# A two-layer decoder trunk: the modulation loads of both feed-forwards move from SyncE's DMA queue to GpSimd's

## The chip, the cores and the metric

The kernel runs on one core of a Trainium2 chip. The metric is the device time of one execution in microseconds (us), the median of several runs. A profile is one further execution, recorded by the hardware profiler; its own time is given beside its span.

## The reference

Two layers work on x (512 positions, 1024 features, float32). The first mixes positions by stick-breaking attention, the second by attention over 128 keys that an indexer selects; each is followed by a gated feed-forward with a causal convolution of width 3. Each of the four sub-layers is normalised, shifted, scaled and gated by vectors that come from one condition vector c:

```python
cond = silu(c)
for i in range(2):
    mod = cond @ ada_w[i] + ada_b[i]                 # 1024 x 6144
    sh1, sc1, g1, sh2, sc2, g2 = split(mod, 6)
    h = rms_norm(x, norm_mix[i]) * (1 + sc1) + sh1
    x = x + g1 * (stick_breaking(h) if i == 0 else dsa(h))
    h = rms_norm(x, norm_ffn[i]) * (1 + sc2) + sh2
    u = conv3(h @ ffn_w_up[i]) + conv_b              # 512 x 5632
    gate, val = split(u, 2)
    x = x + g2 * ((silu(gate) * val) @ ffn_w_down[i])
```

The product `cond @ ada_w[1]` of the second layer is what the moved loads feed.

## The kernel before, in words

Activations are kept transposed: features lie on the 128 partitions, the 512 positions along the free axis. All weights lie in one array `wst` of chunks of 128 x 1024 float32, 512 KB each. A weight is used as the sum of a high part (rounded to a shorter float format, by ScalarE) and a low part (the rest); TensorE multiplies high by high, high by low and low by high. So each chunk is loaded as `raw` (`chunk_raw`, L613, on SyncE's queue, six buffers) and split: ScalarE copies it into `whi`, and then either VectorE subtracts into `wlo` (L653, L1535), or ScalarE writes the negated high part and GpSimd issues a DMA that adds the chunk from memory to it (L662, `add_up` L1543, `add_half` L1554, `add_down` L1732). GpSimd issues other accumulating DMAs too (L1579, L1714, L1752). GpSimd's engine does nothing else in a feed-forward.

The modulation of the second layer is not computed by TensorE. For each of 48 columns a chunk `ada` is loaded, and VectorE multiplies it by `cond` (the same on all partitions) and sums along the row (`dot`, which calls `ada_dot`, L722). 33 of these dots are run in the first layer's feed-forward and 8 in that of the second (`FFN_DOTS`), where the gate that they make is wanted only by the down projection's additions; the other 7 are run elsewhere and are not touched. In a feed-forward the tile `ada` has one buffer, so a load waits until the dot before has read it.

The order of a feed-forward's instructions is set by a planner (`ffn_plan`): it holds jobs with an engine, a duration, what they come after and when they are due, plays them forward with one queue per engine, and `ffn_layer` then calls the functions of class `do` in the order of the planned starts. A load is there a job of SyncE's (`load`), an accumulation one of GpSimd's; the dots are due at equal distances (`DOT_SPAN`). Each engine runs its own instructions in the order in which they were called. Ahead of the planned part stand the first columns of the up projection (`pt_first`, then `pt_u`, L1622 and L1626), whose four last accumulations are issued at L662. TensorE's later products are `pt_a`, `pt_b` and `pt_d` (L1649, L1653, up) and `pt_d` (L1741, down). What a product has written is read by ScalarE (L1489) and, for the convolution, twice by VectorE (L1494), which frees its bank; three banks serve `pt_u`.

Of the kernel before, what the change touches and what calls it, by code (L numbers as in the profile page):

```python
# [525 lines left out]
def chunk_order():  # L526
    keys = []
    for l in range(DEPTH):
        for g in range(6):
            keys += [("ada", l, g, k) for k in range(KT)]  # L530
    for p in range(PAIRS):
        keys += [("q", p), ("k", p)]
    for g in range(4):
        keys += [("v", g, h) for h in range(2)]
    for nm in ("o", "do"):
        for g in range(2):
            keys += [(nm, g, m) for m in range(4)]
    for l in range(DEPTH):
        for j in range(FT):
            keys += [("up", l, j, 0), ("up", l, j, 1)]  # L540
        for r in range(3):
            keys += [("dn", l, r, m) for m in range(KT)]
        keys += [("dn", l, 3, m) for m in range(4)]
    keys += [("qi", i) for i in range(4)] + [("kw",), ("lat",)]
    keys += [("dq", h) for h in range(HEADS)]
    keys += [("uv",)]
    keys += [("bt", n, i) for n in range(3) for i in range(2)]
    return {k: i for i, k in enumerate(keys)}


CH = chunk_order()
# [22 lines left out]
def kernel_body(ctx, tc, xT, wst, cst, smalls, crow, ccol, relb, outT):  # L574
    nc = tc.nc
    act, dve, pe, pool = nc.scalar, nc.vector, nc.tensor, nc.gpsimd
# [900 lines left out]
    def ffn_layer(l, first, man):  # L1477
        with ExitStack() as st:
# [3 lines left out]
            A, R, W, Y, dn, pt, T, half, t1, whole, t4s = {}, {}, {}, {}, {}, {}, {}, {}, {}, {}, {}  # L1482
# [41 lines left out]
            class do:  # L1524
# [240 lines left out]

                def load_ada(*d):
                    R[d] = fp.tile([P, D], F32, name="ada", bufs=1)
                    nc.sync.dma_start(R[d], wst[CH[("ada",) + d]])

                def dot(n, g, f):  # L1770
                    ada_dot(mod[n][:, g * KT + f:g * KT + f + 1], R[n, g, f])
# [816 lines left out]
```

## Time and profile before

| | |
|---|---|
| time, median of 3 runs | 1208.68 us (1208.6 to 1208.86) |
| the profiled execution | 1209.77 us, span 1208.0 us |
| granted TensorE clock | 1.000 |
| busy: TensorE | 1201.4 us, 99% |
| busy: VectorE, ScalarE, GpSimd | 1021.0, 804.7, 240.2 us |
| DMA moved | 226.73 MB, mean 188 GB/s |
| first feed-forward | about 279 to 583 us |
| second feed-forward | about 882 to 1205 us |

A row of a timeline gives the start and the duration in us, the engine, the line, the operation, the tile written and those read, how many like instructions were merged, and in brackets the idle time before it and what ended that. SPq is SyncE's queue, where DMAs are issued; POOL is GpSimd. A row of issues gives the size of each DMA and the median time from issue to landing. A row of waits gives the total, the number and the longest.

### The profile page before, as it was taken

How to read it: one execution, taken by the hardware profiler on the slowest of the kernel's cores; microseconds unless marked ns; L12 is line 12 of the kernel's file. 1: busy time of each engine (PE TensorE's matmuls, PEld its weight loads, DVE VectorE, ACT ScalarE, POOL GpSimd, SP SyncE). 2: the span in 40 equal slices, each digit the busy share in tenths (PEclk: the TensorE clock that was granted, in tenths of full speed). 3: DMA queues.
4: the chain of work that ended last, by engine and by line, in shares of the span. 5: the costliest groups of instructions: out<-in, count | busy, mean ns of one | idle time of the engine just before them, and what ended most of it. 6: DMA issues, size and time to landing. Idle time of an engine off the chain costs nothing.

```text
span 1208.0 us, 18307 instructions
## 1 busy us (share of the span) xinstructions
PE 1201.4 (99%) x6500; PEld 1006.1 (83%) x6500; DVE 1021.0 (85%) x1739; ACT 804.7 (67%) x1393; POOL 240.2 (20%) x284
## 2 busy tenths in 40 slices
PE   9999999999999999999999999999999999999998
PEld 6888788788898998898888778777888888888887
DVE  5898888988999988999798895678989898888883
ACT  5588786368666676666567458774786677677660
POOL 0001100001111111111000457881012122212110
PEclk9999999999999999999999999999999999999999
DMA  9778897629789898896611362346498888788662
GB/s 374 253 204 230 219 250 236 205 90 227 185 221 277 223 250 215 239 273 167 192 53 40 99 156 67 101 129 190 137 236 203 228 186 205 183 182 191 157 147 87
DMA packets 82947, 226.73 MB, mean 188 GB/s; under 512 B 16924, under 2 KB 20252, under 8 KB 82856
## 3 DMA queue, kind: packets, MB, share of 16 engines
q1 hardware_dynamic: 61920, 170.21, 43.1%
q0 software_dynamic: 20912, 55.33, 25.9%
q8 instruction: 51, 0.84, 0.3%
q14 instruction: 40, 0.33, 0.1%
q10 hardware_dynamic: 24, 0.02, 0.0%
HBM read 212.62 MB, written 2.16 MB: 178 GB/s over the span
## 4 chain that ended last, share of the span: by engine, by line
PE 92%; DMA 3%; DVE 1%; POOL 1%; issue 1%; ACT 1%; SPq 0%; POOLq 0%; DVEq 0%; ACTq 0%
PE pt_d L1741 16%; PE pt_a L1653 8%; PE pt_u L1622 6%; PE pt_a L1649 5%; PE pt_d L1653 4%; PE pt_u L1626 3%; PE pt_d L1649 3%; PE pt_l L694 2%; PE pt_l L696 2%; PE pt_l L695 2%; PE pt_qk L694 2%; PE pt_qk L696 2%; PE pt_qk L695 2%; PE pt_b L1653 2%; DMA raw<-wst 2%; PE pt_fv L1099 2%
## 5 line engine op out<-in xcount | busy, mean ns | idle before, releaser
L1741 PE MATMUL pt_d<-actlo,dnhi 128*128 128x512 f32 x288 | 112.8, 392 | 0.0
L1741 PE MATMUL pt_d<-acthi,dnhi 128*128 128x512 f32 x288 | 112.7, 391 | 0.0
L1531 ACT ACTIVATE whi<-raw 128x1024 fp32r<-128x1024 f32 x72 | 75.8, 1054 | 30.0 <-PE pt_a L1653 13.3
L644 ACT ACTIVATE whi<-raw 128x1024 fp32r<-128x1024 f32 x80 | 84.2, 1052 | 4.8 <-DMA raw<-wst 2.0
L662 POOL DMA_DIRECT2D wlo<-wst x23 | 19.9, 864 | 282.3 <-DVE hh L806 131.3
L1622 PE MATMUL pt_u<-hh,whi 128*128 128x512 f32 x320 | 75.8, 389 | 0.0
L1741 PE MATMUL pt_d<-acthi,dnlo 128*128 128x512 f32 x288 | 73.5, 391 | 0.0
L1622 PEld LDWEIGHTS pt_u<-hh,whi 128*128 128x128 f32 x320 | 60.0, 188 | 12.6 <-issue 0.2
L1543 POOL DMA_DIRECT2D wlo<-wst x37 | 32.2, 869 | 169.7 <-ACT wlo L1539 65.5
L1741 PEld LDWEIGHTS pt_d<-actlo,dnhi 128*128 128x128 f32 x288 | 54.2, 188 | 10.2
L1741 PEld LDWEIGHTS pt_d<-acthi,dnhi 128*128 128x128 f32 x288 | 54.2, 188 | 10.1
L1741 PEld LDWEIGHTS pt_d<-acthi,dnlo 128*128 128x128 f32 x288 | 53.1, 188 | 10.3
L1649 PE MATMUL pt_a<-hh,whi 128*128 128x512 f32 x228 | 61.4, 391 | 0.1
L1349 DVE TENSOR_TENSOR_SCAN mz<-mz,diag 128x768 f32<-128x768 f32 (+1 forms) x32 | 47.6, 1486 | 15.1 <-ACT mz L1343 14.9
L1653 PE MATMUL pt_a<-hh,wlo 128*128 128x256 f32 x360 | 57.4, 282 | 0.0
L1653 PEld LDWEIGHTS pt_a<-hh,wlo 128*128 128x128 f32 x360 | 53.1, 190 | 4.5
L722 DVE SCALAR_TENSOR_TENSOR raw<-raw,cond 128x1024 f32<-128x1024 f32 x46 | 54.8, 1219 | 1.4 <-ACT cond L1167 1.3
L1964 DVE CUSTOM_DVE_ANT_0 L<-z,L,cols 128x128 f32<-128x128 f32 (+3 forms) x60 | 32.4, 547 | 27.2 <-PE tr L2267 17.6
L653 DVE TENSOR_TENSOR wlo<-raw,whi 128x1024 fp32r<-128x1024 f32 x42 | 51.6, 1228 | 3.3 <-ACT whi L644 2.9
L1554 POOL DMA_DIRECT2D whi<-wst x30 | 26.0, 866 | 132.3 <-ACT whi L1551 76.0
L722 DVE SCALAR_TENSOR_TENSOR ada<-ada,cond 128x1024 f32<-128x1024 f32 x41 | 49.9, 1218 | 2.5 <-DMA ada<-wst 2.5
L694 PE MATMUL pt_q<-hh,whi 128*128 128x512 f32 x128 | 51.8, 405 | 0.0
(423 smaller groups left out, 3796.7 us busy)
## 6 DMA issues: line engine op xcount, KB each, us to landing
raw<-wst SPq DMA_DIRECT2D x215, 512.0 KB, 5.3
wlo<-wst POOLq DMA_DIRECT2D x60, 512.0 KB, 7.9
ada<-wst SPq DMA_DIRECT2D x45, 512.0 KB, 4.2
raw<-wst SPq DMA_DIRECT2D x48, 384.0 KB, 5.0
whi<-wst POOLq DMA_DIRECT2D x30, 256.0 KB, 5.8
dnlo<-wst POOLq DMA_DIRECT2D x16, 384.0 KB, 7.0
x<-xt POOLq DMA_DIRECT2D x18, 256.0 KB, 5.8
th<-relb SPq DMA_DIRECT2D x16, 256.0 KB, 3.9
```

The costliest lines, as they stand in the source:

```text
L644: act.activation(hi[:, :n], raw[:, :n], AF.Copy)
L653: engine.tensor_sub(lo[:, :w], raw[:, :w], hi[:, :w].bitcast(F32))
L694: pe.matmul(out, lhsT=whi, rhs=ahi, start=start, stop=False)
L695: pe.matmul(out, lhsT=wlo, rhs=ahi, start=False, stop=False)
L696: pe.matmul(out, lhsT=whi, rhs=alo, start=False, stop=stop)
L722: dve.scalar_tensor_tensor(raw, raw, 1.0, cond, op0=OP.mult, op1=OP.mult, accum_out=dst)
L1349: dve.tensor_tensor_scan(rev, rev, diag[:, b:e][:, ::-1], 0.0, OP.mult, OP.max)
L1531: act.activation(W[j, i][0], R[j, i], AF.Copy)
L1622: pe.matmul(pt[j, i], lhsT=W[j, i][0][:, k * P:(k + 1) * P], rhs=hs[k][n], start=k + n == 0, stop=False)
L1649: pe.matmul(pt[j, bank, "both"], lhsT=w[:, c0 + k * P:c0 + (k + 1) * P], rhs=a[2], start=new and k == 0, stop=False, skip_group_check=True)
L1653: pe.matmul(out, lhsT=w[:, c0 + k * P:c0 + (k + 1) * P], rhs=a[n], start=new and k + n == 0, stop=part == 1 and k == 3 and what in ("a2", ...
L1741: pe.matmul(pt["dn", i], lhsT=dn[i][part][:, k * P:(k + 1) * P], rhs=A[j0 + k][n], start=part + k + n == 0, stop=part == 1 and k == j1 - j ...
```

## The change

One line changes: the loads of the modulation weights in both feed-forwards are issued on GpSimd's queue.

```diff
                 def load_ada(*d):
                     R[d] = fp.tile([P, D], F32, name="ada", bufs=1)
-                    nc.sync.dma_start(R[d], wst[CH[("ada",) + d]])
+                    pool.dma_start(R[d], wst[CH[("ada",) + d]])
```

The planner is not changed: it still holds the load as a job of SyncE's, so the sequence in which all functions are called stays as it was, and the 41 loads stand in GpSimd's order where they fall in that sequence. TensorE, VectorE and ScalarE have the same rows as before; GpSimd's and SyncE's differ.

GpSimd at the beginning of the first layer's feed-forward, before (`wlo` at L662 are the last accumulations ahead of the planned part, at L1543 those of the columns that follow, `ha` and `actlo` accumulations of activations):

```order
L662 DMA wlo_2761<-wst 128x1024
L662 DMA wlo_2774<-wst 128x1024
L1543 DMA wlo_2886<-wst 128x1024
L1543 DMA wlo_2906<-wst 128x1024
L1579 DMA ha_2950<-hh_2384 128x512
L1714 DMA actlo_2981<-y1_2889 128x512
L1543 DMA wlo_3027<-wst 128x1024
L1543 DMA wlo_3074<-wst 128x1024
L1543 DMA wlo_3126<-wst 128x1024
```

and now:

```order
L662 DMA wlo_2761<-wst 128x1024
L662 DMA wlo_2774<-wst 128x1024
L1768 DMA ada_2794<-wst 128x1024
L1768 DMA ada_2891<-wst 128x1024
L1543 DMA wlo_2886<-wst 128x1024
L1543 DMA wlo_2906<-wst 128x1024
L1579 DMA ha_2950<-hh_2384 128x512
L1714 DMA actlo_2981<-y1_2889 128x512
L1543 DMA wlo_3027<-wst 128x1024
L1543 DMA wlo_3074<-wst 128x1024
L1768 DMA ada_3087<-wst 128x1024
L1543 DMA wlo_3126<-wst 128x1024
```

The first two modulation loads stand between the last accumulation of L662 and the first of L1543; the second of them waits for the first dot.

SyncE at the beginning of the second layer's feed-forward, before (`raw` are raw weights at L613):

```order
L613 DMA raw_9167<-wst 128x1024
L1768 DMA ada_9204<-wst 128x1024
L613 DMA raw_9223<-wst 128x1024
L613 DMA raw_9225<-wst 128x1024
L613 DMA raw_9227<-wst 128x1024
L613 DMA raw_9229<-wst 128x1024
L613 DMA raw_9239<-wst 128x1024
L613 DMA raw_9258<-wst 128x1024
L1768 DMA ada_9288<-wst 128x1024
```

and GpSimd there now:

```order
L662 DMA wlo_9171<-wst 128x1024
L662 DMA wlo_9184<-wst 128x1024
L1768 DMA ada_9204<-wst 128x1024
L1768 DMA ada_9288<-wst 128x1024
L1543 DMA wlo_9296<-wst 128x1024
L1543 DMA wlo_9316<-wst 128x1024
L1768 DMA ada_9344<-wst 128x1024
```

The first load stood ahead of six raw loads on SyncE; on GpSimd it stands behind the accumulations of L662. SyncE's rows are otherwise the same without the `ada` loads.

## The prediction

> **What bounds the kernel now.** I read the page first (busy time, then the chain that ended last), then the busy time and the waits of the two stretches in which the moved loads run, 279 to 583 us and 889 to 949 us, then the two queues around them. The first two rows are from the page; the table has its columns in its first row.
>
> ```profile
> PE 1201.4 (99%) x6500; PEld 1006.1 (83%) x6500; DVE 1021.0 (85%) x1739; ACT 804.7 (67%) x1393; POOL 240.2 (20%) x284
> PE 92%; DMA 3%; DVE 1%; POOL 1%; issue 1%; ACT 1%; SPq 0%; POOLq 0%; DVEq 0%; ACTq 0%
> ...
> core 0: us, PE busy (x) PEld busy (x) DVE busy (x) ACT busy (x) POOL busy (x), PEclk, DMA share, GB/s
> 279.00:583.00 304.00, 303.26 (x1794) 270.00 (x1793) 273.63 (x428) 204.30 (x308) 47.65 (x55) 1.00 0.86 230
> 889.00:949.00 60.00, 60.00 (x272) 49.91 (x271) 54.05 (x89) 41.42 (x60) 10.45 (x12) 1.00 0.87 223
> ```
>
> TensorE is the bound: 99% busy over the span, and in the two stretches idle for 304.00 - 303.26 = 0.74 us and 0. So nothing is left there to be won, and every microsecond for which TensorE waits is added to the end. VectorE is 90% busy in both (30.4 us idle of 304), and the DMA engines 86 and 87%. Now the waits (us in total, times, longest): TensorE's only one in the first stretch (none was found from 880 to 950 us), SyncE's longest there, and VectorE's for the moved loads in the whole run.
>
> ```profile
> PE pt_d L1649 <- DVE vx L1689: 0.6, 1, 0.6
> ...
> SPq L1768 <- DVE ada L722: 142.3, 25, 11.2
> SPq L613 <- ACT wlo L1539: 18.4, 2, 14.1
> ...
> DVE ada L722 <- DMA ada<-wst: 2.5, 3, 2.0
> ```
>
> The modulation tile `ada` has one buffer, so SyncE stands at each load (L1768) until the dot before (L722) has read the tile, 142.3 us in 25 waits, and issues at once. The time in which the load must land is the distance from one dot's end to the next dot's start, on a VectorE that works in order. At three places:
>
> ```profile
> 355.05 0.08 DVE L722 DVE_READ_ACCUMULATOR ada<-ada,cond 128x1 f32 x1
> 355.16 0.33 SPq L1768 DMA_DIRECT2D ada<-wst  x1
> 359.63 1.22 DVE L722 SCALAR_TENSOR_TENSOR ada<-ada,cond 128x1024 f32<-128x1024 f32 x1
> ...
> 572.77 0.08 DVE L722 DVE_READ_ACCUMULATOR ada<-ada,cond 128x1 f32 x1
> 576.74 1.22 DVE L722 SCALAR_TENSOR_TENSOR ada<-ada,cond 128x1024 f32<-128x1024 f32 x1
> ...
> 918.54 0.08 DVE L722 DVE_READ_ACCUMULATOR ada<-ada,cond 128x1 f32 x1
> 922.85 1.22 DVE L722 SCALAR_TENSOR_TENSOR ada<-ada,cond 128x1024 f32<-128x1024 f32 x1
> ```
>
> These leave 4.47, 3.9 and 4.2 us. Of the 39 loads that follow a dot of their own stage, 15 have under 6.0 us (from the one for 359.63 to the one for 922.85, both above); at a landing time of 5.0, 6.0 and 7.0 us the missing times add up to 3.3, 13.2 and 30.1 us.
>
> **The change part by part.** It moves 41 loads of 512 KB from SyncE's queue to GpSimd's; no byte and no arithmetic is added. How long such a load takes from GpSimd the trace doesn't show. The nearest rows are the issues between 279 and 583 us (KB of each, median us to landing):
>
> ```profile
> raw<-wst SPq DMA_DIRECT2D x42, 512.0 KB, 6.7
> ada<-wst SPq DMA_DIRECT2D x32, 512.0 KB, 4.2
> wlo<-wst POOLq DMA_DIRECT2D x21, 512.0 KB, 7.3
> whi<-wst POOLq DMA_DIRECT2D x15, 256.0 KB, 6.5
> ```
>
> *Landing time.* Lower bound 4.2 us, the same load by SyncE. Upper bound 7.3 us, a transfer of this size by GpSimd that also accumulates. Half the bytes save GpSimd's transfers only 0.8 us (7.3 to 6.5), so most of the 7.3 is the queue and what stands in it, which a load without accumulation shares. I take 6.0, a little above the middle (5.75). The Trainium skill ("DMA: Bandwidth & Descriptors", section on one DMA by the software path) fits 2.0 us plus the bytes at 436 GB/s, an estimated 3.2 us for 512 KB; no row of GpSimd's at this size is near it here, and by it the moved loads would be no later than now, which is the first rival's case.
>
> *The first load of each feed-forward.* Now it is issued long ahead; after the change it stands behind the four accumulations of the boundary (L662) and ahead of the first two of the layer (L1543). The rows are SyncE's, GpSimd's, the dot's, the two VectorE rows that free the bank, and TensorE's next product, for the first layer and then for the second; the last row is the landing of all L662 transfers.
>
> ```profile
> 268.66 0.33 SPq L1768 DMA_DIRECT2D ada<-wst  x1
> 286.17 0.87 POOL L662 DMA_DIRECT2D wlo<-wst  x1 [2.36 <-ACT wlo L661]
> 292.69 1.22 DVE L722 SCALAR_TENSOR_TENSOR ada<-ada,cond 128x1024 f32<-128x1024 f32 x1
> 293.83 2.97 DVE L1494 SCALAR_TENSOR_TENSOR y<-pt_u,sm,y 128x511 f32<-128x511 f32 x4
> 295.57 3.82 PE L1622 MATMUL pt_u<-hh,whi 128*128 128x512 f32 x16
> ...
> 871.21 0.33 SPq L1768 DMA_DIRECT2D ada<-wst  x1
> 885.80 0.87 POOL L662 DMA_DIRECT2D wlo<-wst  x1 [8.06 <-ACT wlo L661]
> 889.02 0.86 POOL L662 DMA_DIRECT2D wlo<-wst  x1 [2.36 <-ACT wlo L661]
> 893.40 1.22 DVE L722 SCALAR_TENSOR_TENSOR ada<-ada,cond 128x1024 f32<-128x1024 f32 x1
> 896.08 1.52 DVE L1494 SCALAR_TENSOR_TENSOR y<-pt_u,sm,y 128x511 f32<-128x511 f32 x2
> 898.24 3.79 PE L1622 MATMUL pt_u<-hh,whi 128*128 128x512 f32 x16
> ...
> DMA to landing us min/median/max: 6.3/8.0/10.4
> ```
>
> First layer: the last L662 transfer, issued at 286.17, lands at about 294.2 (8.0 later). The modulation load is issued when GpSimd is free, 286.17 + 0.87 = 287.0. If the queue serves in order it lands about 1 us behind its predecessor, at 295.2, and the dot starts 2.5 us late. The product at 295.57 needs the bank that the first two L1494 free, 293.83 + 2.97 / 2 = 295.3: slack 0.2, so TensorE loses **2.3 us**. Not held by its predecessor, it lands at 287.0 + 4.2 = 291.2 and costs nothing; at 6.0 it would be 0.3 late. Second layer, likewise: 889.02 + 8.0 + 1 = 898.0 against 893.40, 4.6 late; the two L1494 end at 897.6, 0.6 before the product at 898.24: **4.0 us**. Its lower end is 0 (889.9 + 4.2 = 894.1, within the slack). I take both full values: the last two L662 there were issued 3.2 us apart (885.80 and 889.02) against 8.0 to land, so the queue is not empty when the load comes.
>
> *The loads inside the layers.* At 6.0 us the 15 short intervals make VectorE wait for 13.2 us (12 of them, 9.9 us, in the first layer). VectorE has 30.4 us of idle time there to make it good, but it comes between the dots and TensorE has none, so what is behind a late dot (convolutions that free banks, low parts of weights) is late for the product that follows closely. Between nothing and all of it I take half: **6 us**. At 5.0 us the full sum is 3.3, at 7.0 it is 30.1.
>
> *What queues behind the waiting load.* GpSimd now stands at the second load until the first dot has ended, and these two have been issued behind it:
>
> ```profile
> 291.81 0.87 POOL L1543 DMA_DIRECT2D wlo<-wst  x1 [4.78 <-ACT wlo L1539]
> 294.37 0.86 POOL L1543 DMA_DIRECT2D wlo<-wst  x1 [1.70 <-ACT wlo L1539]
> 301.04 3.34 PE L1622 MATMUL pt_u<-hh,whi 128*128 128x512 f32 x14
> ```
>
> The late dot ends at 295.2 + 1.2 + 0.1 = 296.5; the load issues, and 0.87 later the accumulations, at 297.4 and 298.3 in place of 291.81 and 294.37. The first would land near 297.4 + 7.3 = 304.7. Its product begins at 301.04 + 2.3 with the high part, 16 matmuls or 3.8 us as at 295.57, so it is wanted at about 307.1: 2.4 us of margin, **0**; without that margin the excess would come on top, up to 3 us at the queue's longest landing times. GpSimd's own 41 x 0.87 = 36 us of issuing fits into its idle time (47.65 busy of 304). On SyncE the raw weights (L613) lose the 142.3 us of waiting ahead of them. They land earlier, which TensorE can't use beyond its 0.74 us: **0**.
>
> Sum: 2.3 + 4.0 + 6 = 12.3 us. The profiled execution took 1209.77 us around its span of 1208.0, so 1222.1 for it; it lies 1.09 above the median of the runs, 1208.68, on which the same sum gives **1221 us**.
>
> **The rivals.**
> *The load lands as fast as from SyncE.* If it takes at most 4.5 us and isn't held by its predecessors, three intervals fall short, by 1.0 us in all, and both first loads arrive within the slack. The time is 1208.7 to 1210, not slower. For it: the loads without accumulation have less to do per byte, and on SyncE they take 4.2 at the median though 86% of the DMA engines is busy. Against: every GpSimd row of 256 KB or more is above it. The page of the Trainium skill named above gives this result; its section on the two kinds of descriptor generation sends plain loads to SyncE or ScalarE for the quicker setup, which by itself would speak for a small loss.
> *GpSimd's queue blocks both ways.* At 7 us and more, loads and accumulations wait for each other: the dot's wait moves the next load, and that the accumulations behind it. The missing time is 30.1 us at 7.0, most of it beyond VectorE's idle time; with the 6.3 of the two starts it gives 1208.7 + 6.3 + 20 to 43, so 1235 to 1258. For it: DMA at 86%, and 7.3 for the accumulations. Against: a plain load moves less.
> *Faster.* SyncE's raw loads, freed of the dots' waits, end TensorE's wait of 0.6 us and what else of the 0.74 hangs on them: 1208 us. It can't reach 0.2% (2.4 us), about what a measurement of this kernel tells from no change.
>
> **How the numbers follow.** My forecast 0.66, with its own range 1213 to 1231 (landing times of 5.0 to 6.5, starts between half and full price); landing as from SyncE 0.14; blocking both ways 0.17; faster 0.03. The first and the third of these are slower by over 0.2%: 0.83; the second is within it: 0.14; faster 0.03. The range reaches to 1211, half the price of both starts with a few late dots at the lower end, and to 1237, the cheap part of the blocking.
>
> **What would show it.** Right: the modulation load lands 5 to 7 us after its issue; the first dots of the layers start 2 to 3 and 4 to 5 us later after the layer's beginning, with TensorE waits of that size on VectorE just behind; VectorE's wait for the moved loads grows from 2.5 us to 10 to 25; SyncE's waits on L722 are gone and GpSimd has them. Wrong: a landing time at 4 us; or late dots with TensorE's idle time unchanged (then VectorE's slack took them all); or a TensorE wait on the accumulated low parts, which I priced at 0.

## The result, and the profile after

The changed kernel takes 1222.97 us (median of 4 runs, 1220.84 to 1223.59) against 1208.67 before: a ratio of 1.0115, 95% interval 1.0097 to 1.0132, so 14.3 us more. The profiled execution took 1223.42 us around a span of 1221.6. The moved loads' issues between 279 and 592 us (KB, median us to landing) and, of the whole run, VectorE's and TensorE's waits (us in total, times, longest) and GpSimd's for the dots:

```profile
ada<-wst POOLq DMA_DIRECT2D x33, 512.0 KB, 6.0
wlo<-wst POOLq DMA_DIRECT2D x21, 512.0 KB, 7.5
...
DVE ada L722 <- DMA ada<-wst: 23.3, 15, 5.9
...
PE pt_u L1622 <- DVE sm L1614: 5.4, 1, 5.4
PE pt_u L1622 <- DVE y L1494: 2.6, 1, 2.6
PE pt_a L1649 <- DVE vx L1689: 1.4, 2, 0.8
...
POOL ada L1768 <- DVE ada L722: 102.0, 24, 10.4
```

The load lands after 6.0 us at the median where it took 4.2; VectorE waits for it 23.3 us where it was 2.5; and TensorE, which had one wait of 0.6 us in the feed-forwards, now has four that sum to 9.4. Two of them stand at the starts of the layers. GpSimd's issues, the late dot, the convolutions behind it and TensorE's next product, first and second layer:

```profile
286.77 0.86 POOL L662 DMA_DIRECT2D wlo<-wst  x1 [2.37 <-ACT wlo L661]
287.46 0.73 POOL L1768 DMA_DIRECT2D ada<-wst  x1
296.06 1.23 DVE L722 SCALAR_TENSOR_TENSOR ada<-ada,cond 128x1024 f32<-128x1024 f32 x1 [2.69 <-DMA ada<-wst]
297.21 2.97 DVE L1494 SCALAR_TENSOR_TENSOR y<-pt_u,sm,y 128x511 f32<-128x511 f32 x4
298.89 5.50 PE L1622 MATMUL pt_u<-hh,whi 128*128 128x512 f32 x16 [2.55 <-DVE y L1494]
...
894.83 0.86 POOL L662 DMA_DIRECT2D wlo<-wst  x1 [2.36 <-ACT wlo L661]
895.69 0.57 POOL L1768 DMA_DIRECT2D ada<-wst  x1
905.17 1.23 DVE L722 SCALAR_TENSOR_TENSOR ada<-ada,cond 128x1024 f32<-128x1024 f32 x1 [5.89 <-DMA ada<-wst]
907.87 1.53 DVE L1494 SCALAR_TENSOR_TENSOR y<-pt_u,sm,y 128x511 f32<-128x511 f32 x2
909.54 6.15 PE L1622 MATMUL pt_u<-hh,whi 128*128 128x512 f32 x16 [5.36 <-DVE sm L1614]
```

The two loads land 8.6 and 9.5 us after their issue, 1.2 and 1.3 us behind the accumulation that GpSimd had issued 0.7 us before the first and 0.9 us before the second. Counted from their layer's first product the two dots start 2.8 and 6.0 us later than before, and TensorE stands for 2.55 and 5.36 us. (The second wait's row names `sm`, a small operation that VectorE ran right behind the two convolutions; the product itself reads only `hh` and `whi`.) And something that the prediction did not have: the 16 products that follow take 5.50 and 6.15 us where the same line took 3.8 before. The windows show why (us, busy of PE, PEld, DVE, ACT and POOL, then the granted clock):

```profile
300.00:304.00 4.00, 4.00 (x13) 3.10 (x12) 3.96 (x9) 1.04 (x2) 0.86 (x1) 0.58 0.93 184
304.00:308.00 4.00, 4.00 (x19) 3.32 (x18) 3.00 (x4) 2.81 (x5) 0.00 (x0) 1.00 1.07 207
909.00:911.00 2.00, 1.46 (x4) 1.21 (x5) 1.97 (x5) 0.63 (x1) 0.06 (x1) 0.50 0.93 201
911.00:913.00 2.00, 2.00 (x6) 1.63 (x5) 1.97 (x4) 0.00 (x0) 0.55 (x1) 0.50 0.93 164
```

Just behind each stand the granted clock is 0.5: 3.4 us long from 300.0, and 6.8 us from 907.5 by the trace's clock record. The products lose 5.50 - 3.79 = 1.7 and 6.15 - 3.79 = 2.4 us by it, half of the 3.4 and 4.8 us for which TensorE worked at that clock.

Where the profiled executions spent their time, cut at the first and the last matmul of `pt_u` and the last of `pt_d` in each layer (us; worked out from the starts and ends of those matmuls):

| stage | before | after | first by SyncE | only first | only 2nd layer's | same, filled | four by SyncE |
|---|---|---|---|---|---|---|---|
| up, first columns, layer 1 | 54.59 | 59.00 | 54.61 | 58.67 | 54.61 | 54.58 | 54.56 |
| rest of that feed-forward | 249.45 | 250.08 | 252.19 | 248.21 | 248.21 | 248.87 | 248.21 |
| up, first columns, layer 2 | 54.57 | 62.48 | 54.56 | 62.24 | 60.74 | 59.34 | 54.57 |
| rest of that feed-forward | 245.81 | 245.81 | 245.81 | 245.81 | 245.81 | 245.81 | 245.81 |
| span | 1207.95 | 1221.63 | 1211.20 | 1218.44 | 1212.55 | 1211.57 | 1206.58 |

After minus before: 4.4 and 7.9 us at the two starts, 0.6 in the rest of the first layer, none in that of the second; the other 0.7 of the 13.7 us between the spans lies ahead of the first layer (0.6) and between the two. The rest of the first layer is 248.21 us where TensorE has no wait; the profile before took 1.2 us more, around its one wait, and that of after 1.9 more. Of all runs, one (in the experiment with one load alone) took 1312.58 us at a mean granted clock of 0.851, and no ratio counts it.

### The profile page after: what moved, and what is told of

Read it like the earlier page. It is cut to its first block, busy times and chain, and to the rows that moved or that the text cites. A ratio compares the mean times of both kernels' runs of the same rounds, so it can differ in the third digit from the quotient of the medians.

```text
span 1221.6 us, 18294 instructions
## 1 busy us (share of the span) xinstructions
PE 1205.8 (99%) x6500; PEld 1008.5 (83%) x6500; DVE 1021.3 (84%) x1739; ACT 805.2 (66%) x1393; POOL 263.2 (22%) x325
## 4 chain that ended last, share of the span: by engine, by line
PE 88%; issue 4%; DMA 3%; DVE 2%; POOL 2%; ACT 1%; SPq 0%; POOLq 0%; ACTq 0%; DVEq 0%
PE pt_d L1741 15%; PE pt_a L1653 8%; PE pt_a L1649 5%; PE pt_u L1622 5%; PE pt_d L1653 4%; DMA ada<-wst 3%; PE pt_d L1649 3%; PE pt_l L694 2%; PE pt_l L696 2%; PE pt_l L695 2%; PE pt_qk L694 2%; PE pt_qk L696 2%; PE pt_qk L695 2%; PE pt_u L1626 2%; PE pt_b L1653 2%
## 5 line engine op out<-in xcount | busy, mean ns | idle before, releaser
L1622 PE MATMUL pt_u<-hh,whi 128*128 128x512 f32 x320 | 79.9, 404 | 7.9 <-DVE sm L1614 5.4
L1622 PEld LDWEIGHTS pt_u<-hh,whi 128*128 128x128 f32 x320 | 62.7, 197 | 22.1 <-issue 5.8
L662 POOL DMA_DIRECT2D wlo<-wst x23 | 19.9, 864 | 282.4 <-DVE hh L806 131.3
L722 DVE SCALAR_TENSOR_TENSOR ada<-ada,cond 128x1024 f32<-128x1024 f32 x41 | 50.1, 1221 | 23.3 <-DMA ada<-wst 23.3
L1741 PEld LDWEIGHTS pt_d<-acthi,dnlo 128*128 128x128 f32 x288 | 53.1, 188 | 10.3
L1768 POOL DMA_DIRECT2D ada<-wst x41 | 24.4, 596 | 135.2 <-DVE ada L722 102.0
L1543 POOL DMA_DIRECT2D wlo<-wst x37 | 32.2, 879 | 93.4 <-ACT wlo L1539 51.6
```

Source lines behind the costliest of these rows:

```text
L722: dve.scalar_tensor_tensor(raw, raw, 1.0, cond, op0=OP.mult, op1=OP.mult, accum_out=dst)
L1622: pe.matmul(pt[j, i], lhsT=W[j, i][0][:, k * P:(k + 1) * P], rhs=hs[k][n], start=k + n == 0, stop=False)
L1741: pe.matmul(pt["dn", i], lhsT=dn[i][part][:, k * P:(k + 1) * P], rhs=A[j0 + k][n], start=part + k + n == 0, stop=part == 1 and k == j1 - j ...
```

## The experiments

The theory (A) was by now: the two first loads make the loss, by the stand and by the clock behind it. The rivals: the 39 loads inside the layers (B), the accumulations held behind a waiting load (C), GpSimd's queue being slow wherever the load stands (D). Ratios are to the kernel before, in runs on the same chip.

**The first loads back on SyncE's queue.**

```diff
-                    pool.dma_start(R[d], wst[CH[("ada",) + d]])
+                    queue = nc.sync if d in (DOTS[4], DOTS[40]) else pool
+                    queue.dma_start(R[d], wst[CH[("ada",) + d]])
```

> Only the first modulation load of each feed-forward goes back to SyncE's queue; the other 39 stay on GpSimd's. Theory A (the two starts make the loss: 2.55 and 5.36 us of idle TensorE in the profile after, and the slower granted clock just behind each): about 1208.7 + 0.8 + 0.6 of idle time inside the layers = 1210, at most 1211. Rival B (the loads inside the layers make it, as the 6 us of the prediction's third term had it): 1214 to 1216.

1213.91 us (1212.98 to 1214.55), ratio 1.0041 (1.0026 to 1.0056): 5.1 us over the 1208.83 of the kernel before. The starts cost nothing any more (54.61 and 54.56 us), so they made 9 of the 14.3 us; but the loads inside cost more than the 1.4 that A read off the profile after, and nearly what B said. Both had a part. TensorE's waits between 279 and 583 us, and the place of the longer one, VectorE then TensorE:

```profile
PE pt_a L1649 <- DVE vx L1689: 3.5, 2, 2.7
...
569.05 1.22 DVE L722 SCALAR_TENSOR_TENSOR ada<-ada,cond 128x1024 f32<-128x1024 f32 x1 [3.59 <-DMA ada<-wst]
570.20 0.41 DVE L1689 TENSOR_TENSOR vx<-vx,pt_a 128x256 f32<-128x256 f32 x1
...
570.67 1.20 PE L1649 MATMUL pt_a<-hh,whi 128*128 128x512 f32 x4 [2.74 <-DVE vx L1689]
```

This dot waits 3.59 us, and the next operation of VectorE is the one that TensorE needs: 2.74 us arrive there. VectorE waited for the load 12 times in this run, 15.4 us, but only two places reach TensorE.

**Only the first loads moved.**

```diff
+                    queue = pool if d in (DOTS[4], DOTS[40]) else nc.sync
+                    queue.dma_start(R[d], wst[CH[("ada",) + d]])
```

> Only the first modulation load of each feed-forward is on GpSimd's queue; the other 39 are SyncE's again, so GpSimd never waits for a dot. Theory A: 2.55 + 5.36 us of idle time and 1.7 + 2.4 us of slower clock behind them: 1208.7 + 12.0 = 1220.7 (1219 to 1222). Rival B (loads inside the layers): about 1215. Rival C (the accumulations held behind the second load make TensorE late at the starts): near 1209, since nothing is held here.

1219.81 us (1219.39 to 1220.39), ratio 1.0090 (1.0075 to 1.0106): A, 0.9 below its figure. The stands are 2.3 and 4.6 us, with the clock at 0.5 for 3.4 and 6.8 us behind them as in the whole change. Rival C falls: GpSimd waits for no dot here, nothing is held back, and the starts take 58.67 and 62.24 us against 59.00 and 62.48. This run's 11.0 and the 5.1 of the run before make 16.1, more than the 14.3 of the whole change: there the two places inside cost TensorE waits of 0.78 and 0.64 us, where they cost 0.79 and 2.74 in the run before. Why the late starts make the second place cheaper was not followed up.

**Only the second layer's first load moved.**

```diff
+                    queue = pool if d == DOTS[40] else nc.sync
+                    queue.dma_start(R[d], wst[CH[("ada",) + d]])
```

> Only one load of all, the first of the second layer's feed-forward, is on GpSimd's queue. Theory A: 5.36 us of idle time and 2.4 us of slower clock: 1208.7 + 7.8 = 1216.5 (1215.5 to 1217.5). If the clock did not count: 1214.

1214.65 us (1214.38 to 1214.91), ratio 1.0048 (1.0031 to 1.0065): 5.8 us for one load of 41. Less than the 7.8 expected, as the stand was 4.3 us in place of 5.36 and the clock was at 0.5 for one piece of 3.4 us and not for two. 4.32 + 1.7 = 6.0 is what the stage lost (60.74 less 54.57 makes 6.2).

**All on GpSimd's queue, the first one earlier.** The tile is made and the load issued where the layer begins, ahead of the last two accumulations of L662; the planned call is left out.

```diff
             pts, vs = first
+            d = FFN_DOTS[l][0]
+            R[d] = fp.tile([P, D], F32, name="ada", bufs=1)
+            pool.dma_start(R[d], wst[CH[("ada",) + d]])
             es = [evac_scale(0, i, vs[i]) for i in range(2)]
...
                 def load_ada(*d):
+                    if d in R:
+                        return
```

> All 41 loads stay on GpSimd's queue, but the first of each feed-forward is called at the layer's beginning, ahead of the last two accumulations of the boundary (L662). Theory A (the load is late because it stands behind these): the starts cost nothing, 1209 to 1211 as with the first load on SyncE. Rival D (a load from GpSimd is slow by itself, wherever it stands): the starts are late as before, 1219 to 1223.

1212.68 us (10 runs, nine from 1211.0 to 1213.89 and one of 1220.96), ratio 1.0036 (1.0021 to 1.0052). The starts are whole again (54.61 and 54.56 us), with every load on GpSimd's queue; D falls, and what is left is the price inside (253.20 and 246.25 us in the rests of the two layers), as with the first loads on SyncE. GpSimd's issues at the beginning of the first layer; the last row is the second modulation load, behind the first dot:

```profile
273.88 0.86 POOL L662 DMA_DIRECT2D wlo<-wst  x1 [2.27 <-ACT wlo L661]
274.66 0.64 POOL L1504 DMA_DIRECT2D ada<-wst  x1
282.82 0.86 POOL L662 DMA_DIRECT2D wlo<-wst  x1 [7.52 <-ACT wlo L661]
294.10 0.55 POOL L1773 DMA_DIRECT2D ada<-wst  x1 [7.19 <-DVE ada L722]
```

The load still stands 0.8 us behind an accumulation, and by the landing record it takes 8.0 us here too; it only starts 12.8 us sooner (274.66 for 287.46). So the load isn't late for being on this queue, but for being issued late behind an accumulation. The slow landing has its part in the loss all the same: 4.2 us after its issue at 287.46 the load of the whole change would have landed at 291.7, ahead of the 293.4 at which the dot stood ready.

The issue and landing records of all profiles show what the slow landing comes from. From 279 us on, the profile after has 136 transfers of GpSimd's that were issued while the one before them was still on its way; each landed behind that one, by 0.9 us or more, and in the other profiles too none came out of order. The nine moved loads that found all earlier transfers landed took 4.2 us at the median (4.0 to 5.4), no more than from SyncE; the other 32 took 6.7 (3.8 to 10.6). A first load of a layer that was issued just behind an accumulation landed 1.2 to 1.3 us behind it, in all ten cases. So what a plain load pays on this queue is mostly what stands ahead of it.

This run also shows the clock inside a layer: after a stand of 1.95 us,

```profile
570.05 1.95 PE L1652 MATMUL pt_a<-hh,whi 128*128 128x512 f32 x4 [1.95 <-DVE vx L1692]
...
570.00:574.00 4.00, 3.95 (x12) 3.33 (x13) 3.14 (x6) 0.63 (x1) 0.52 (x1) 0.57 0.89 242
```

the four matmuls take 1.95 us where they took 1.20 in the run above, whose stand of 2.74 us was followed by none of it. The one run of 1220.96 had a mean clock of 0.996 against 0.999 to 1.000 of the others; what fell there can't be seen, as it left no trace.

**The stand filled.** Products that nobody reads are put on TensorE just ahead of the product that waits, 9 in the first layer and 20 in the second.

```diff
                     if j < 4:
                         W[j, i] = chunk(("up", l, j, i), 0)
+                    if (j, i) == (3, 1):
+                        spare_bank = ptile([P, S], "pt_fill", "tr")
+                        for _ in range((9, 20)[l]):
+                            pe.matmul(spare_bank, lhsT=W[j, i][0][:, :P], rhs=hs[0][0], start=True, stop=True)
```

> The changed kernel, with products that nobody reads (9 in the first layer, 20 in the second, about 0.23 us each, into a free bank) put on TensorE just ahead of the product that waits at each start (2.55 and 5.36 us). They leave the computation as it is and lie inside the waits. Theory A (the granted clock falls to 0.5 behind the idle time, 3.4 and 6.8 us long, and costs 1.7 and 2.4 us): the clock stays at 1.0 there and the time falls by about 4.1, to 1219. Rival E (the slow clock has another cause, or what follows is bound by VectorE and not by the clock): no change, 1222 to 1224.

1221.16 us, but spread from 1217.94 to 1225.16, ratio 1.0104 (1.0084 to 1.0125). In the profiled execution (1219.66) the clock stays at 1.0 throughout and the starts take 57.44 and 59.10 us, 4.9 less than in the change; the rest of the first layer takes 251.83. Two runs kept a mean clock of 1.0 (1217.94, 1219.66), two had 0.998 and 0.997 (1222.65, 1225.16), so in these the clock fell somewhere, and they left no trace. The median doesn't decide it; hence a cleaner run, with nothing moved but the second layer's first load.

**The stand filled, one load moved.** The kernel of the third experiment, with 16 such products in the second layer.

```diff
+                    if (l, j, i) == (1, 3, 1):
+                        spare_bank = ptile([P, S], "pt_fill", "tr")
+                        for _ in range(16):
+                            pe.matmul(spare_bank, lhsT=W[j, i][0][:, :P], rhs=hs[0][0], start=True, stop=True)
```

> As the run in which only the first load of the second layer is on GpSimd's queue (1214.65; 4.3 us of idle time and 3.4 us at half the clock behind it), with 16 products that nobody reads (3.6 us) put into that idle time; the computation is as it was. Theory A (idle time lowers the granted clock, and that costs 1.9 us): the clock stays at 1.0, the up products of that layer take 58.9 us in place of 60.7, and the time is 1212.8. Rival E (the clock has another cause or is not the bound): 1214.7.

1213.61 us (5 runs, 1212.88 to 1214.58), ratio 1.0041 (1.0028 to 1.0053): 1.0 less than without the products (0.7, each against its own runs of the kernel before), half of what was expected or less. The two intervals overlap, so what follows rests on the rows and the stage, from one profile each. TensorE in the profile without them and with them, each with the granted clock of the four microseconds from 902:

```profile
901.55 5.49 PE L1622 MATMUL pt_u<-hh,whi 128*128 128x512 f32 x16 [4.32 <-DVE sm L1614]
...
902.00:906.00 4.00, 4.00 (x13) 3.11 (x12) 3.53 (x7) 0.13 (x1) 0.00 (x0) 0.57 0.49 150
```

```profile
897.52 3.79 PE L1622 MATMUL pt_fill<-hh,whi 128*128 128x512 f32 x16
902.18 3.89 PE L1626 MATMUL pt_u<-hh,whi 128*128 128x512 f32 x16 [0.88 <-DVE sm L1614]
...
902.00:906.00 4.00, 3.82 (x17) 3.20 (x18) 3.54 (x8) 0.63 (x1) 0.00 (x0) 1.00 0.41 166
```

More work on TensorE, the wait ending as late as before (21.0 us after the layer's first product, 20.8 without), and the product is done 1.6 us sooner in its own time (3.89 for 5.49) because the clock was kept. In the stage it is 59.34 for 60.74, 1.4 us. So idle time lowers the clock and the clock costs; that VectorE bounds the products behind the wait falls. Part of the gain is missing from the time because the first layer has a wait of its own (248.87 for 248.21), at 484 us, where the profile before has one too.

**Two more loads back.** The first experiment's kernel, with the two loads whose dots stand ahead of its two places at 387 and 567 us.

```diff
-                    queue = nc.sync if d in (DOTS[4], DOTS[40]) else pool
+                    queue = nc.sync if d in (DOTS[4], DOTS[40], DOTS[13], DOTS[34]) else pool
```

> As the run with the two first loads on SyncE, and two more of the first layer's loads with them: those whose dots stand just ahead of the two places where TensorE still waited there (387 and 567 us, 0.8 and 2.7 us; their dots had waited 1.6 and 3.6 us). 37 loads stay on GpSimd's queue. Theory G (a late dot costs only where TensorE closely follows, and these are the two places): 1208.7 to 1210. Rival H (the lateness of many dots adds up on VectorE, whichever load it is): 1212 to 1214 as without it.

1208.85 us (11 runs, 1208.64 to 1211.16), ratio 1.0005 (0.9996 to 1.0014): no difference from the kernel before, with 37 of the 41 loads on GpSimd's queue. G holds, H falls:

```profile
DVE ada L722 <- DMA ada<-wst: 12.5, 12, 2.5
```

VectorE still waits 12 times for 12.5 us, five times the 2.5 of before, and TensorE has no wait at all between 279 and 583 us.

**One load alone**, the one whose dot waited 2.0 us ahead of TensorE's only wait in the profile before.

```diff
+                    queue = pool if d == DOTS[24] else nc.sync
+                    queue.dma_start(R[d], wst[CH[("ada",) + d]])
```

> The kernel before, with one of the 41 loads alone on GpSimd's queue: the one whose dot waited 2.0 us at 480 us in the profile before (it landed 8.0 us after its issue, beside raw loads), just ahead of TensorE's only wait in the feed-forwards (0.6 us). If that load's landing makes the wait: 0.6 to 1.2 us faster, 1207.6 to 1208.2. If the raw weights that land late at the same place make it: no change, 1208.7.

1208.74 us (11 runs, ten from 1208.05 to 1209.57), ratio 0.9999 (0.9990 to 1.0008): nothing gained. In its profile the load landed 6.0 us after its issue in place of 8.0, and TensorE had no wait there; but two other profiles with that load on SyncE's queue have no wait there either (the table's 248.21 with only the first loads moved), so the 0.6 us come and go without it.

**The planner told.** The first experiment's kernel, in which the planner knows where the other 39 loads are issued and that they land later.

```diff
-                got, raw = load("load_ada", *d, ring="ada", key=due)
+                issue = p.add("POOL", 0.87, "load_ada", *d)
+                got, raw = p.add("DMA", 1.45 * 1.11, None, after=[issue], lag=4.0), p.place("ada", issue, due)
```

> As the run with the first loads on SyncE, but the planner is told that the other 39 are jobs of GpSimd's with 0.87 us to issue, and a landing 5.6 us later, so it moves the dots and their neighbours on VectorE. Theory A (the price inside the layers is the dots standing where a load by SyncE would have landed): most of its 5 us goes, 1209 to 1211. Rival F (any load on this queue delays the accumulations that TensorE needs): 1213 to 1215 as without it.

1233.82 us (1233.09 to 1235.38), ratio 1.0209 (1.0195 to 1.0223): both theories missed. VectorE's waits for the load fell to five, but TensorE now waits for ScalarE at other places. The first three rows are of the whole run; the last four are from the second layer, up to the longer wait:

```profile
DVE ada L726 <- DMA ada<-wst: 11.5, 5, 4.6
...
PE pt_d L1745 <- ACT xt L1753: 6.9, 1, 6.9
PE pt_d L1745 <- ACT dnhi L1726: 5.3, 1, 5.3
...
970.73 1.22 DVE L726 SCALAR_TENSOR_TENSOR ada<-ada,cond 128x1024 f32<-128x1024 f32 x1
971.99 0.17 DVE L730 TENSOR_TENSOR mod<-mod,sm 128x8 f32<-128x8 f32 x1
972.19 0.69 ACT L1753 ACTIVATE xt<-pt_d,mod 128x512 f32<-128x512 f32 x1 [2.10 <-DVE mod L730]
972.93 0.80 PE L1745 MATMUL pt_d<-acthi,dnhi 128*128 128x512 f32 x1 [6.88 <-ACT xt L1753]
```

The wait of 6.9 us hangs on the dots: the planner put the second layer's last dot 74.4 us behind the layer's first product, where it stood 65.6 us behind it before. Its sum `mod` is ready only then, ScalarE scales a finished product of the down projection by it, and TensorE waits for that. What made the wait of 5.3 us was not followed up. The planner moved far more than the dots, so this run doesn't tell what the late landings cost.

No version was found that is faster than the kernel before.

## Why the prediction was right, point by point

- **The bound.** TensorE had no slack to give, and each microsecond of its waiting came out at the end: shown by the two starts, which lose what TensorE waits and what the clock takes, to 0.2 us (2.55 + 1.7 of 4.4, 5.36 + 2.4 of 7.9).
- **The landing time.** Taken as 6.0, between 4.2 and 7.3; measured 6.0 at the median. The weighing of rows by the same queue against rows by the same kind of load held. The 6.0 is a mixture: 4.2 for the nine loads that found the queue empty, 6.7 for the others. So the rival "lands as fast as from SyncE" describes those nine and falls for the rest. (One of its readings is a little off: at 4.5 us the second layer's first dot would have been 1.0 us late against a slack of 0.6, so that start would have cost 0.3.) The fit of the Trainium skill ("DMA: Bandwidth & Descriptors", section "Anatomy of one DMA") gives an estimated 3.2 us; the trace does not agree here, 3.8 at the least and 6.0 at the median, with the DMA engines 86% busy.
- **The starts.** Priced 2.3 and 4.0 us, with TensorE's waits measured at 2.55 and 5.36. The mechanism is shown: with these loads elsewhere or earlier the starts cost nothing, with them alone the starts cost nearly the same, and the dots' lateness of 2.8 and 6.0 us less the predicted slack of 0.2 and 0.6 gives the two waits. The second was mis-sized in its landing: I put it 1 us behind a predecessor that lands after 8.0; the predecessor landed after 9.0 and the load 1.3 behind it, 10.3 in all (894.83 to 905.15). The 1 us had no row behind it, but was near: 1.2 to 1.3 in ten cases.
- **What was missing.** The sum held no term for the granted clock. It fell to 0.5 behind both stands and cost 1.7 and 2.4 us. With it the starts cost 4.4 and 7.9 us in place of 2.3 and 4.0. The Trainium skill has the rule ("TensorE: Matmul & The Clock Gate", Part 1): half the clock after an idle window of about 3.4 us, full clock again after a busy one, windows that run freely. The pieces of 3.4 and 6.8 us agree with its window, and within a profile all changes of the clock lie whole multiples of 3.413 us apart. But a window needn't be idle throughout. Cut along that grid, the eleven profiles (their first 7 us and their ends apart) have nine windows at full clock in which TensorE idled for 1.95 us or more, and half the clock followed each of them; the next idlest had 1.82 us, and full clock followed it and all others. So how long a stand may be depends on where it falls: the one of 1.95 us lay in one window, the one of 2.74 us was cut into 1.14 and 1.60 and cost no clock.
- **The loads inside.** Priced 6 us, as half of the 13.2 that VectorE would wait. Alone they cost 5.1, beside the starts 1.9 in the profile. But "half" was a guess at a spread, and the spread is not there: two of the 39 loads carry the whole price, where the next operation on VectorE is one that TensorE waits for; the other 37 cost nothing, though 12 dots still waited, 12.5 us in all. The right size alone was partly luck. So was the total: in the whole change the waits at the starts were 7.9 us for 6.3 priced, the clock took 4.1 for nothing priced, and inside it was 1.9 for 6, so the too large third term made good for the missing clock.
- **What queues behind.** Priced 0. In the run without any waiting on GpSimd the starts were 0.3 and 0.2 us shorter, so it is near 0 there.
- **The rivals.** The queue that blocks both ways didn't come about: GpSimd waited 102 us for dots, and no TensorE wait is on an accumulated part. (The 43 us of its upper price had no working.) The faster case had 0.6 us to win, and the change lost elsewhere.

## What to carry to other kernels

When a transfer moves to another queue, look first at the loads that were issued long ahead: they lose their lead and land behind whatever stands in the new queue. One load of 41 made 5.8 us here. For the loads in a steady stretch, don't share their lateness out evenly; ask of each what the engine does next and whether the bound engine waits for that. And where TensorE is the bound, price its stand with the slower clock behind it: 2.55 us idle cost 4.4, 5.36 cost 7.9, and 2.74 at another place cost no clock.

## What the runs showed of the hardware

- A plain 512 KB load takes GpSimd 0.56 us to issue at the median, an accumulation of the same size 0.86 to 0.88 (the profile after); GpSimd's issue followed the end of the dot by 0.30 us, where SyncE's followed by 0.03.
- A plain 512 KB load by GpSimd's queue landed after 4.2 us at the median when the queue was empty (nine loads of the profile after), and after 7.6 to 9.5 when it stood within a microsecond behind an accumulation (the first loads of the layers, ten in six profiles), 1.2 to 1.3 us behind it. Transfers of this queue landed in the order of their issue in every profile. How much of these times comes from other transfers on the same DMA engines was not tested apart.
- The granted clock falls to 0.5 in pieces of 3.4 us, on a grid of 3.413 us, behind a window of that grid in which TensorE idled for 1.95 us or more (nine of nine) and behind none with 1.82 us or less. From these numbers it is an estimate that a single stand under 1.8 us keeps the clock, and one over 3.9 us loses it wherever it falls.
